# First projection columns by quarters, a reordered end, pairwise squares and moved copies in a one-core decoder step

## The chip, the core and the metric

The kernel runs on one core of one Trainium2 chip (trn2). A core has a matrix engine (TensorE, "PE", with its weight loads listed apart as "PEld"), a vector engine (VectorE, "DVE"), a scalar engine (ScalarE, "ACT"), a general engine (GpSimd, "POOL") and a queue that only issues transfers (SyncE, "SP"). Each engine works through its own instructions in order, and they meet through semaphores. ACT and POOL issue transfers as well. The metric is the device time of one execution in microseconds (us); the profiled execution's span, from its first to its last instruction, is a little shorter.

## The reference

One step of a decoder layer over 512 prompt tokens and 32 sample tokens (8 sequences of 4), 544 tokens of 1024 features, all in float32:

```python
h = RMSNorm_pre(x)
[x_r | q | k | v | g] = h @ W_in                 # 1024 -> 1024 + 1024 + 256 + 256 + 2048
A = RG-LRU(causal_conv4(x_r))                    # recurrent branch, gates by 8 diagonal blocks
B = sliding-window(128) attention, 8 query heads, 2 kv heads, sinks, relative bias
m = (sigmoid(g_A) * (A @ W_A) + sigmoid(g_B) * (B @ W_B)) @ W_out
x = x + RMSNorm_post(m)
u = causal_conv3(RMSNorm_pre2(x) @ W_up)         # 1024 -> 8192
x = x + RMSNorm_post2((gelu(u_gate) * u_val) @ W_down)   # 4096 -> 1024
```

It returns the new x of both groups, the recurrent states, the last keys and values, and the last rows before both convolutions.

## The kernel before

Features lie on the 128 partitions and tokens along the free dimension, so an activation is a set of tiles of 128 x 544. Every product is made exact enough by splitting both operands into a high part (ACT rounds it) and a low part (DVE subtracts it), and by three matmuls: high by high, high by low, low by high. Tokens go in two halves: 256 and 288 (`HALF`), from the output projection on 272 and 272 (`HALF2`). A column block is 128 outputs, with 8 blocks of the inner dimension: 24 matmuls for each half.

**The order.** PE, ACT, DVE and POOL instructions run in the order in which the program writes them (in the second part POOL, too, is ordered by a scheduler); SP's are placed by priority. In the mixer `step` makes one half column, and then `tick` advances a clock `now` and emits what is due: generators put in with `start_at(t, ...)`, the results of the step before (`late`), the weight splits that `wclaim` names (ACT part `wsplit_hi`, DVE part `wsplit_lo`), and last the list `last`.

**The start.** POOL builds `ident` and then `ones`; 7 warm-up matmuls (14 passes on PE, L403) use both. The first 256 tokens arrive as four tiles of 128 x 512 and the first weight column in two halves of its inner dimension. `trans_a(z)` (L469) transposes four of the eight feature blocks on PE, `hsplit` (L445, L446) scales and splits them, and `first_step` (L1024) makes the first half column from the first four blocks, then from the other four. `keep_a` and `keep_b` (L454) copy the transposed tokens out, and `trans_b` (L487) brings tokens 256 to 543. The other five of the first six columns follow for half 0, then all six for half 1, then the other six. `ATTN` gives the ticks of the 16 attention units.

**The second norm.** `norm_chain(1, acc)` runs beside the first up-projection products ("pq", with weight splits "wl_e"). In five groups, half a tick apart, it scales two blocks, adds them to x (POOL, or DVE for blocks 5 and 7), squares them on ACT (L1257), and `sum_up` adds seven squares of 128 x 272 one after the other to `accx` on DVE (L174).

**The pairs.** Each of the up-projection's 32 column pairs from 6 on takes seven products of 12 matmuls ("s", a Strassen-like form: a11, a12, p2, p3, p1, p4, a22). Its weight sums are made by DVE and by two adding transfers of POOL (L1433, L1434). Between them stand halves of the down-projection ("dn", q = 0 to 6), at the places that the planner names: behind a12, p3, p1 and a22, and in pairs 29 to 31 behind p1 and a22. A transfer named ("up", p, "s") brings the weights of one pair a second time; for pairs 30 and 31 (`APART_S`) it goes into two slots from the pool of 52 (L1402).

**The end.** The last quarter of the down-projection (`QL`) runs for half 1 and then half 0. `last_done` adds the result, squares it on ACT (L1775) and collects the squares. `b_sums`, `b_scale`, `b_spread`, `b_norm`, `rows` and `b_out` norm half 1 beside half 0's products and write it out by token blocks 2 to 4. For half 0, `last_sums` and `last_newton` give the row scale, and `a_out` (L1828) scales, adds the tokens of before and writes; its block (1, 1) goes by ACT (L1832) and POOL (L1833).

Of the kernel before, what the change touches and what calls it, by code (L numbers as in the profile page):

```python
# [17 lines left out]
P = 128  # L18
# [34 lines left out]
APART_S = 30  # L53
E_BUFS = 5
# [4 lines left out]
NORM_TICKS = (3, 1.5)  # L59
# [64 lines left out]
def hawk_step(ctx, tc, I, O):  # L124
# [87 lines left out]

    ident = keep.tile([P, P], F32, name="ident")
    make_identity(nc, ident)
    ones = keep.tile([P, P], F32, name="ones")
    pool.memset(ones, 1.0)
# [14 lines left out]
    qkv_order = (16, 18, 8, 9, 10, 11, 17, 19, 12, 13, 14, 15)  # L231
# [8 lines left out]
    in_slots = {("out", c) for c in range(3, 8)} | {("in", c) for c in qkv_order[3:FIRST]}  # L240
    wraw, wunits, wnext = {}, {}, [0]
# [4 lines left out]
    def wraw_parts(i, us):  # L246
        for u in us:
            nc.sync.dma_start(out=wraw[i][:, 4 * u:4 * u + 4, :], in_=wsrc(order[i])[:, 4 * u:4 * u + 4, :])

    def wload(i, halves=None):  # L250
        key = order[i]
        raw = wraw[i] = rp.tile([P, KD, P], F32, tag="raw", name="raw_" + wname(i))
        if halves is not None:
            wraw_parts(i, halves)
        elif key[0] == "wg":
# [33 lines left out]

    def upto(key, a, look):  # L290
        return 2 * (wpos[key] + look) + a + 1
# [29 lines left out]
    def mmhalf(ps, key, X, a, ks=range(KD), js=range(3)):  # L321
        n = X.half[a][1] - X.half[a][0]
        if key == order[0]:

            for j, (i0, i1) in enumerate(((0, 0), (0, 1), (1, 0))):
                if j not in js:
                    continue
                for k in ks:
                    mm(ps[:, :n], wunits[2 * wpos[key] + k // 4][i0][:, k % 4, :], X.get(k, a, i1),
                       j == 0 and k == 0, j == 2 and k == KD - 1)  # L330
            return
        for k in ks:
            wh, wl = (wunits[2 * wpos[key] + k // 4][j][:, k % 4, :] for j in range(2))
            xh, xl = X.get(k, a, 0), X.get(k, a, 1)
            mm(ps[:, :n], wh, xh, k == 0, False)
            mm(ps[:, :n], wh, xl, False, False)
            mm(ps[:, :n], wl, xh, False, k == KD - 1)
# [34 lines left out]

    relx = cp.tile([NBK + 1, NH], F32, name="relx")
    ohp = T("ohp")[:NBK + 1, 0:3 * WIN]
    pool.memset(relx, 1.0)
    xload(0, 0)
    xload(1, 0)
    wload(0, (0,))
    xload(0, 1)
    xload(1, 1)  # L380
    wraw_parts(0, (1,))
    wload(1)
    nc.sync.dma_start(out=ohp, in_=I["c_ohp"])
    nc.sync.dma_start(out=relx[0:NBK, :], in_=I["rel_bias"])
    wload(2)
    for z in range(2):
        for i in (2, 3, 4):
            xload(i, z)
        wload(3 + z)
    wload(5)  # L390
# [12 lines left out]
    for z in range(WARM):  # L403
        mm(pw[:, (z % 4) * P:(z % 4 + 1) * P], ones, ident, True, True)
# [14 lines left out]
    for k in range(KD):  # L419
        h.alloc(k)  # L420
    ss = cp.tile([P, 4, 5], F32, name="ss")
    dve.memset(ss, 1.0)
# [7 lines left out]
    def xsquares(i, zs=(0, 1)):  # L430
        n = TOK[i][1]
        for z in zs:
            xb = xt[i, z][:n, 0:512]
            if z == 0:
                act.activation(jk[:n, 0:512], xb, AF.Square, accum_out=ss[:n, 0, i:i + 1])
            else:
                dve.scalar_tensor_tensor(out=jv[:n, 0:512], in0=xb, scalar=1.0, in1=xb, op0=ALU.mult,
                                         op1=ALU.mult, accum_out=ss[:n, 1, i:i + 1])

    def xtile(i, k):  # L440
        return xt[i, k // 4][:, (k % 4) * P:(k % 4 + 1) * P]
# [22 lines left out]
    def trans_a(z):  # L464
        for i in range(2):
            for j in range(4):
                if j not in pta:
                    pta[j] = (PM if j == 3 else PX)(f"ps_ta{j}")
                pe.transpose(pta[j][:, z * 256 + i * P:z * 256 + (i + 1) * P], xtile(i, 4 * z + j), ident)  # L469

    def split_a(z, ks):
        for j in ks:
            hsplit(4 * z + j, 0, pta[j][:, z * 256:(z + 1) * 256])

    def keep_a(j):
        xkeep(slice(j, KD, 4), 0, 256, pta[j][:, 0:512], act.copy if j % 2 else dve.tensor_copy)
# [6 lines left out]
    def trans_b(ks):  # L483
        for k in ks:
# [3 lines left out]
            hsplit(k, 1, ps[:, :288])  # L488
        for k in ks:
            keep_b(k)  # L490

    def side_b():
        for ks in (range(0, 3), range(3, 6), range(6, 8)):
            last.append(lambda ks=ks: trans_b(ks))
            yield
        yield
        xspill()

    def roots():
        add(ss[:, 0, :], ss[:, 0, :], ss[:, 1, :])  # L500
# [6 lines left out]
    def row_scales():  # L507
        last.extend(lambda i=i: xsquares(i, (1,)) for i in range(2))
        yield 2
        last.append(lambda: xsquares(2))  # L510
        yield
        last.extend(lambda i=i: xsquares(i) for i in (3, 4))
        yield
# [164 lines left out]
    def kv_done(kv, a, ps, nm, scaled):  # L678
# [5 lines left out]
        if a == 1:  # L684
# [3 lines left out]
            late.append(scale)  # L688
# [305 lines left out]

    start_at(3, side_b())
    start_at(3, row_scales())
    start_at(4, once(xspill))
    start_at(2, row_loads())
    start_at(3, attn_tables())
    start_at(9, params())  # L1000
    start_at(14, cache_shift())
    for hp in range(4):
        start_at((7, 12, 19, 27)[hp], once(load_btab, hp))
    start_at(12, sample_tables())
# [19 lines left out]
    def first_step():  # L1024
        key = order[0]
        ps = PM("pm_first")
        def parts(z):
            split_a(z, range(1))
            lows = [wsplit_hi(w) for w in wclaim(z + 1)]
            split_a(z, range(1, 4))  # L1030
            for v in lows:
                wsplit_lo(*v, pool)

        k03, k47 = range(4), range(4, 8)
        trans_a(0)
        parts(0)
        for i in range(2):
            xsquares(i, (0,))
        mmhalf(ps, key, h, 0, k03, (0, 1))
        trans_a(1)  # L1040
        parts(1)
        mmhalf(ps, key, h, 0, k03, (2,))
        mmhalf(ps, key, h, 0, k47)
        last.extend(lambda j=j: keep_a(j) for j in range(4))
        tick(6)
        late.append(lambda: in_done(qkv_order[0])(0, ps))

    first_step()
    table_loads()
    for z, c in enumerate(qkv_order[:FIRST]):  # L1050
        if z:
            step(("in", c), h, 0, in_done(c), target=min(2 * z + 6, 2 * FIRST))
    for z, c in enumerate(qkv_order[:FIRST]):
        step(("in", c), h, 1, in_done(c), target=2 * FIRST + (0, 2, 4, 6, 6, 6)[z])
    for c in qkv_order[FIRST:]:
        for a in range(2):
# [165 lines left out]
    def norm_chain(a, acc):  # L1222
# [8 lines left out]
        with tc.high_priority(offset=HP):  # L1231
# [12 lines left out]
            def sum_up(c):  # L1244
                add(acc2[:, :n], acc2[:, :n], sq[c][:, :n])

            for g in range(5 if a else 0):
# [7 lines left out]
                for c in range(2 * g - 2, 2 * g) if g else ():  # L1255
# [646 lines left out]
```

## Time and profile before

| | |
|---|---|
| median of 3 runs | 996.52 us (996.49 to 996.71) |
| profiled execution, its own time | 996.34 us |
| its span | 994.6 us |
| mean granted PE clock | 0.997 |
| HBM read, written | 111.30 MB, 11.37 MB |
| kernel's share of PE on the chain that ended last | 87% |

The page lists busy time per engine, the chain of work that ended last (followed back from the last instruction), groups of instructions, and transfers. Other views of the same trace give instructions in order of time, waits by pair of engines, and the busy time in any stretch. Ends of PE's instructions are modelled, so a busy PE says less than the starts of its instructions do. A row of the timeline gives start, duration, engine, line, operation, tiles, shape and count, and in brackets the idle time before it with what ended that.

### The profile page before, as it was taken

Reading aid. Unit: us, or ns where it says so; the run is one execution under the profiler, and the core shown is the slowest. Engines: PE = TensorE matmul, PEld = TensorE weight load, DVE = VectorE, ACT = ScalarE, POOL = GpSimd, SP = SyncE. Lnnn points to the kernel's source line nnn. Section 1 sums busy time; section 2 is a strip of 40 time slices with the busy share of each in tenths; the row PEclk is TensorE's granted clock in tenths of the full one; section 3 lists DMA queues with packets and bytes.
Section 4 is the critical chain, followed back from the end, with each engine's and each line's share of the span. In section 5 each row is a group of like instructions: output and inputs, shape, how many; then the busy total and the mean of one; then the engine's idle time right before and its main releaser. Section 6 shows DMA issues by size and latency. Waiting matters only on the chain.

```text
span 994.6 us, 20258 instructions
## 1 busy us (share of the span) xinstructions
PE 981.9 (99%) x7819; PEld 973.3 (98%) x7819; DVE 732.4 (74%) x1547; ACT 596.3 (60%) x1450; POOL 147.4 (15%) x270
## 2 busy tenths in 40 slices
PE   8999999999999999999999999999999999999996
PEld 7999999999999999999999999999999999999996
DVE  5766666685766755589966778787878787879855
ACT  6555556665778635556956655555565655556644
POOL 4242000120101441220001010101010101011003
PEclk9999999999999999999999999999999999999998
DMA  9943223342223634235037586868685868577412
GB/s 269 277 161 94 64 68 105 97 116 64 86 85 86 196 113 140 74 117 165 23 96 180 139 178 141 179 141 180 139 180 140 182 136 182 138 181 196 146 46 91
DMA packets 209236, 134.00 MB, mean 135 GB/s; under 512 B 6696, under 2 KB 195513, under 8 KB 209108
## 3 DMA queue, kind: packets, MB, share of 16 engines
q1 hardware_dynamic: 198548, 110.08, 39.2%
q0 software_dynamic: 10240, 20.08, 11.7%
q10 hardware_dynamic: 352, 2.56, 0.6%
q8 instruction: 61, 1.00, 0.4%
q14 instruction: 35, 0.29, 0.1%
HBM read 111.30 MB, written 11.37 MB: 123 GB/s over the span
## 4 chain that ended last, share of the span: by engine, by line
PE 87%; issue 4%; DVE 4%; DMA 2%; ACT 1%; POOL 1%; POOLq 0%; SPq 0%; DVEq 0%; ACTq 0%
PE pmin L165 22%; PE pmdn L165 18%; PE pux L1513 15%; PE puy L1513 7%; PE pq L1513 6%; PE pmlo L165 4%; PE puz L1513 4%; PE pmao L165 3%; PE pg L165 1%; PE psc L165 1%; PE pvp L165 1%; PE pmout L165 1%; DMA raw_up_s<-in_w_up_dram 1%; DMA raw_up_s<-raw_up_s 1%; DVE accx L174 1%
## 5 line engine op out<-in xcount | busy, mean ns | idle before, releaser
L165 PE MATMUL pmin<-hH,wh_in 128*128 128x256 f32 (+1 forms) x568 | 165.3, 293 | 0.0
L165 PE MATMUL pmin<-hH,wl_in 128*128 128x256 f32 (+1 forms) x568 | 162.8, 289 | 0.3 <-DVE wl_in L288 0.3
L165 PE MATMUL pmin<-hL,wh_in 128*128 128x256 f32 (+1 forms) x568 | 162.5, 288 | 0.0
L165 PE MATMUL pmdn<-fH,wh_dn 128*128 128x256 f32 (+1 forms) x512 | 148.2, 289 | 0.0
L165 PE MATMUL pmdn<-fH,wl_dn 128*128 128x256 f32 (+1 forms) x512 | 147.4, 288 | 0.0
L165 PE MATMUL pmdn<-fL,wh_dn 128*128 128x256 f32 (+1 forms) x512 | 147.3, 288 | 0.0
L165 PEld LDWEIGHTS pmin<-hH,wh_in 128*128 128x128 f32 x568 | 106.9, 189 | 1.3 <-ACT wh_in L283 0.6
L165 PEld LDWEIGHTS pmin<-hL,wh_in 128*128 128x128 f32 x568 | 106.9, 189 | 0.0
L165 PEld LDWEIGHTS pmin<-hH,wl_in 128*128 128x128 f32 x568 | 106.4, 188 | 0.5 <-DVE wl_in L288 0.5
L177 DVE SCALAR_TENSOR_TENSOR uc<-u,fv,uc 128x560 f32<-128x560 f32 x128 | 101.8, 797 | 0.8 <-ACT uc L1544 0.5
L165 PEld LDWEIGHTS pmdn<-fH,wh_dn 128*128 128x128 f32 x512 | 96.5, 189 | 0.1
L165 PEld LDWEIGHTS pmdn<-fL,wh_dn 128*128 128x128 f32 x512 | 96.4, 188 | 0.1
L165 PEld LDWEIGHTS pmdn<-fH,wl_dn 128*128 128x128 f32 x512 | 96.3, 188 | 0.0
L174 DVE TENSOR_TENSOR ft<-ft,pmdn 128x256 f32<-128x256 f32 (+1 forms) x112 | 48.7, 435 | 27.8 <-PE pmdn L165 27.8
L1639 ACT COPY u<-pux 128x272 f32<-128x272 f32 x52 | 20.1, 386 | 80.9 <-PE pux L1513 80.8
L168 DVE TENSOR_TENSOR u<-puy,u 128x240 f32<-128x240 f32 (+2 forms) x78 | 24.6, 344 | 48.5 <-PE puy L1513 31.2
L288 DVE TENSOR_TENSOR wl_in<-raw_in,wh_in 128x512 fp32r<-128x512 f32 x70 | 46.7, 685 | 3.6 <-ACT wh_in L283 3.6
L1544 ACT ACTIVATE uc<-u,fv 128x560 f32<-128x560 f32 x64 | 48.3, 755 | 0.9 <-DVE u L1520 0.9
L168 DVE TENSOR_TENSOR wl_dn<-raw_dn,wh_dn 128x512 fp32r<-128x512 f32 x64 | 43.8, 685 | 4.5 <-ACT wh_dn L1445 4.5
L283 ACT ACTIVATE wh_in<-raw_in 128x512 fp32r<-128x512 f32 x72 | 43.9, 626 | 4.4 <-DMA raw_in<-in_w_in_dram 3.9
L1445 ACT ACTIVATE wh_dn<-raw_dn 128x512 fp32r<-128x512 f32 x64 | 39.7, 623 | 3.0 <-DMA raw_dn<-in_w_down_dram 3.0
L165 PE MATMUL pmout<-mH,wh_out 128*128 128x272 f32 x128 | 37.5, 293 | 0.0
(753 smaller groups left out, 3290.4 us busy)
## 6 DMA issues: line engine op xcount, KB each, us to landing
raw_in<-in_w_in_dram SPq DMA_DIRECT2D x35, 512.0 KB, 4.3
raw_dn<-in_w_down_dram SPq DMA_DIRECT2D x56, 256.0 KB, 3.6
raw_up_s<-in_w_up_dram SPq DMA_DIRECT2D x24, 512.0 KB, 5.7
raw_up_s<-raw_up_s POOLq DMA_DIRECT2D x26, 256.0 KB, 5.4
raw_ao<-in_w_attn_o_dram SPq DMA_DIRECT2D x8, 512.0 KB, 3.9
raw_lo<-in_w_lru_o_dram SPq DMA_DIRECT2D x8, 512.0 KB, 3.8
raw_out<-in_w_out_dram SPq DMA_DIRECT2D x8, 512.0 KB, 5.2
x<-xtd SPq DMA_DIRECT2D x8, 272.0 KB, 6.0
```

What stands on the lines that cost most here:

```text
L165: pe.matmul(out, l, r, start=start, stop=stop)
L168: dve.tensor_tensor(out=out, in0=a, in1=b, op=ALU.subtract)
L174: dve.tensor_tensor(out=out, in0=a, in1=b, op=ALU.add)
L177: dve.scalar_tensor_tensor(out=out, in0=a, scalar=s_, in1=b, op0=op0, op1=op1)
L283: act.activation(hl[0], raw, AF.Copy)
L288: (eng or dve).tensor_tensor(out=hl[1], in0=raw, in1=f32(hl[0]), op=ALU.subtract)
L1445: act.activation(hl[0], src, AF.Copy)
L1513: pe.matmul(ps[:, :HN], w, x, start=start and k == 0 and i == 0, stop=stop and k == 3 and i == 2, skip_group_check=True)
L1544: act.activation(yt[j][:, 0:FLATU], u[:, 0:FLATU], AF.Copy, scale=fv[:, j:j + 1])
L1639: act.copy(e[nm_], z)
```

## The change

1. **Start.** `ones` is made before `ident`, and 6 warm-up matmuls use `ones` alone. The first four projection columns (16 to 19: both keys, both values) are made together for half 0 by quarters of the inner dimension: four transfers of 128 x 2 x 256 for the tokens and four of 128 x 2 x 512 for the weights alternate. For each quarter the four columns' products run part by part, with the next quarter's transposes between them. Three further warm-up matmuls stand behind the first transposes. The first query column then gets half 0 alone, and then half 1 follows for these five columns. Scaling of keys and values gets ticks of its own (`KV_TICK`), the squares of tokens go to `sq4`, and the ticks of the attention units and tables move.
2. **Second norm.** Squares are added by pairs of blocks, 544 wide, and the two halves of the sum at the end.
3. **Last pairs.** The planner's places for pairs 29 to 31 become three, three and one; pair 30's second copy of weights is issued by ACT behind product p3 of pair 28 rather than by SP; three loads of the down-projection go to the slots.
4. **End.** Half 1's last square is added on DVE, so that the column sums take one operand, and they run in the middle of the second product of half 0. Norming, transposes and output of half 1 come one or two steps earlier; the order of the last transposes and outputs is new; the samples' rows leave by ACT's queue.

```diff
+PLACES = (("a12", "p3", "p1", "a22"), ("a12", "p3", "p1"), ("a12", "p3", "p1"), ("a12",))
-NORM_TICKS = (3, 1.5)
+NORM_TICKS = (3, 1)
-FIRST = 6
-ATTN = (10, 12, 14, 16, 18, 20, 22, 24, 26, 28, 30, 32, 34, 36, 38, 40)
+GROUP = (16, 17, 18, 19)
+ATTN = (13, 15, 16, 18, 20, 21, 23, 25, 27, 28, 30, 32, 34, 36, 38, 40)
-WARM = 7
+WARM = 6
+FILL = 3
+KV_TICK = 10
...
-qkv_order = (16, 18, 8, 9, 10, 11, 17, 19, 12, 13, 14, 15)
+qkv_order = (*GROUP, *range(8, 16))
...
+    def gload(q):
+        graw[q] = rp.tile([P, 2, 4 * P], F32, tag="raw", name=f"raw_group{q}")
+        nc.sync.dma_start(out=graw[q], in_=w_in[256 * q:256 * q + 256, GROUP[0] * P:(GROUP[0] + 4) * P]
+                          .rearrange("(k p) n -> p k n", p=P))
...
+    for q in range(4):
+        xquarter(q)
+        gload(q)
+    for i in (2, 3, 4):
+        xload(i, 0)
+    wload(4)
+    for i in (2, 3, 4):
+        xload(i, 1)
...
+    def first_group():
+        accs = [(PX if z == 3 else PM)(f"pm_group{z}") for z in range(4)]
+        def prod(q, z, js):
+            mmhalf(accs[z], order[z], h, 0, (2 * q, 2 * q + 1), js)
+        def splits(q):
+            ghigh(q, 1, dve.tensor_copy if q == 0 else act.copy)
+            ghigh(q, 0, act.copy)
+            lows(q)
+            glow(q, 1, dve)
+            glow(q, 0, dve if q else pool)
+        zs = (2, 3, 0, 1)
+        trans_a(0)
+        warm_up(FILL)
+        highs(0)
+        splits(0)
+        for q in range(4):
+            if q < 3:
+                for z in zs:
+                    prod(q, z, (0,))
+                trans_a(q + 1)
+                highs(q + 1)
+                for z in zs:
+                    prod(q, z, (1,))
+                for z in zs:
+                    prod(q, z, (2,))
+                splits(q + 1)
+                if q == 2:
+                    last.append(lambda: trans_b((0, 1), False))
+                last.append(lambda: keep_a(q))
+                tick(10 if q == 2 else 8)
+                continue
+            for z in zs:
+                prod(q, z, range(3))
+                in_done(GROUP[z])(0, accs[z])
...
-            def sum_up(c):
-                add(acc2[:, :n], acc2[:, :n], sq[c][:, :n])
+            def sum_up(k):
+                add(sq[0], sq[0], sq[k])
+                if k == 3:
+                    add(acc2[:, :n], sq[0][:, 0:n], sq[0][:, n:2 * n])
...
-            for g in range(5 if a else 0):
+            for g in range(6 if a else 0):
...
-                for c in {2: (1,), 3: (2, 3, 4, 5), 4: (6, 7)}.get(g, ()):
-                    sum_up(c)
-                if g < 4:
+                if g > 2:
+                    sum_up(g - 2)
+                if g < 5:
                     yield 0.5
...
-            places = [x for x in todo_ if x[2] in (("p1", "a22") if p_ > 32 - CH else ("a12", "p3", "p1", "a22"))]
+            places = [x for x in todo_ if x[2] in PLACES[max(0, p_ - 28)]]
...
+        if x == ("s", APART_S - 2, "p3"):
+            load(("up", APART_S, "s"), act)
...
+            elif c == 7:
+                add(acc3[1][:, :n], acc3[1][:, :n], sq3[1][7][:, :n])
...
-            down(QL, c, a, last_done(c))
+            down(QL, c, a, last_done(c), b_sums if (a, c) == (0, 1) else None)
...
-    rows(4, 0, PX)
-    rows(0, 0, PM)
+    for i in (2, 3):
+        rows(i, 1, PX)
     while todo:
         slot(0)
-    b_out(4, 0)
+    b_out(2, 1, dve.tensor_copy)
     fin["a"] = last_sums(0, 2, PM("pst_o0"))
-    for i in (2, 3):
-        rows(i, 1, PX)
+    b_out(3, 1)
+    rows(0, 0, PM)
     r = last_newton(*fin["a"])
+    rows(1, 1, PX)
     rows(1, 0, PM)
-    b_out(2, 1)
-    for i in (0, 1):
-        rows(i, 1, PX)
-    b_out(3, 1)
-    a_out(0, 0, r, act)
-    a_out(1, 1, r, nc.sync)
-    a_out(1, 0, r, act)
-    rows(4, 1, PX)
-    b_out(4, 1)
-    a_out(0, 1, r, nc.sync)
+    a_out(0, 0, r)
+    rows(0, 1, PX)
+    a_out(1, 0, r)
+    a_out(1, 1, r)
+    for kk in range(2):
+        rows(4, kk, PX)
+    for kk in range(2):
+        b_out(4, kk)
+    a_out(0, 1, r)
+    for kk in range(2):
+        act.dma_start(out=ys[:, kk * 512:(kk + 1) * 512], in_=fin["o", kk])
```

More of the change, by code (lines that the diff above doesn't have):

```diff
@@ L322, in mmhalf @@
         n = X.half[a][1] - X.half[a][0]
[L323 to L337, printed above, removed]
+        for j_ in (js,) if len(js) == 3 else [(j,) for j in js]:
+            for k in ks:
+                for j, (w, x) in enumerate(((0, 0), (0, 1), (1, 0))):
+                    if j in j_:
+                        mm(ps[:, :n], wpart(key, k, w), X.get(k, a, x), k == 0 and j == 0, k == KD - 1 and j == 2)
     def step(key, X, a, done, target=None, look=2, quick=False):
@@ L402, in hawk_step, with warm_up @@
     ps0 = PX("ps_rows_a0")
-    for z in range(WARM):
-        mm(pw[:, (z % 4) * P:(z % 4 + 1) * P], ones, ident, True, True)
+    def warm_up(n):
+        for z in range(n):
+            mm(pw[:, (z % 4) * P:(z % 4 + 1) * P], ones, ones, True, True)
+    warm_up(WARM)
     pe.transpose(ps0[:, 0:8], rows_a[0:8, :], ident[0:8, 0:8])
@@ L462, in hawk_step, with trans_a, highs, lows @@
     pta = {}
[L464 to L476, printed above, removed]
+    def trans_a(q):
+        pta[q] = PX(f"ps_ta{q}")
+        for z in range(2):
+            for i in range(2):
+                pe.transpose(pta[q][:, z * 256 + i * P:z * 256 + (i + 1) * P], xtile(i, 2 * q + z), ident)
+    def highs(q):
+        for z in range(2):
+            k = 2 * q + z
+            act.activation(h.get(k, 0, 0), pta[q][:, z * 256:(z + 1) * 256], AF.Copy,
+                           scale=pv[:, G_PRE + k:G_PRE + k + 1])
+    def lows(q):
+        for z in range(2):
+            k = 2 * q + z
+            stt(h.get(k, 0, 1), pta[q][:, z * 256:(z + 1) * 256], pv[:, G_PRE + k:G_PRE + k + 1],
+                f32(h.get(k, 0, 0)), ALU.mult, ALU.subtract)
+    def keep_a(q):
+        xkeep(slice(2 * q, 2 * q + 2), 0, 256, pta[q][:, 0:512], act.copy if q % 2 else dve.tensor_copy)
     ptb = {}
@@ L488, in trans_b, with keep_bs @@
             hsplit(k, 1, ps[:, :288])
+        if keep:
+            keep_bs(ks)
+    def keep_bs(ks):
         for k in ks:
             keep_b(k)
[L492 to L497, printed above, removed]
     def roots():
-        add(ss[:, 0, :], ss[:, 0, :], ss[:, 1, :])
+        dve.tensor_reduce(ss[:, 0, :], sq4.rearrange("p z i -> p i z"), AX.X, ALU.add)
         newton_rstd(ss[:, 1, :], ss[:, 3, :], ss[:, 2, :], ss[:, 0, :])
@@ L507, in row_scales @@
     def row_scales():
[L508 to L511, printed above, removed]
+        last.append(lambda: xsquares(0))
+        yield 3
+        for i in (1, 2):
+            last.append(lambda i=i: xsquares(i))
+            yield
         last.extend(lambda i=i: xsquares(i) for i in (3, 4))
-        yield
         last.append(roots)
@@ L687, in scale @@
                 scaled(kv, t_)
-            late.append(scale)
+                yield
+            start_at(KV_TICK + 2 * kv + (nm == "v"), scale())
     def k_scaled(kv, t_):
@@ L1021, in in_done @@
         return lambda a, ps: f(z, a, ps)
[L1024 to L1034, printed above, removed]
-        trans_a(0)
[L1036 to L1046, printed above, removed]
@@ L1048, in hawk_step @@
-    first_step()
-    table_loads()
[L1050 to L1056, printed above, removed]
+    def first_group():
[9 more added lines that the diff above has]
+        zs = (2, 3, 0, 1)
+        trans_a(0)
+        warm_up(FILL)
[20 more added lines that the diff above has]
+                in_done(GROUP[z])(0, accs[z])
+                if z == 3:
+                    keep_bs((0, 1))
+            last.append(lambda: keep_a(q))
+            last.append(lambda: trans_b((2, 3)))
+            tick(10)
@@ L1057, in hawk_step @@
+    first_group()
+    table_loads()
+    c0 = qkv_order[4]
+    ps = PM("pm_first_q")
+    mmhalf(ps, ("in", c0), h, 0, range(4))
+    trans_b((4, 5))
+    mmhalf(ps, ("in", c0), h, 0, range(4, 8))
+    last.append(lambda: trans_b((6, 7)))
+    tick(10)
+    late.append(lambda ps=ps: in_done(c0)(0, ps))
+    for z, c in enumerate(qkv_order):
+        for a in range(1 if z < 5 else 0, 2):
             step(("in", c), h, a, in_done(c))
@@ L1254, in norm_chain @@
                         add(x1_(c), x1_(c), m_)
[L1255 to L1262 removed]
+                if 0 < g < 5:
+                    sq[g - 1] = T(f"sq_x{a}_{g - 1}")[:, 0:2 * n]
+                    for z in range(2):
+                        act.activation(sq[g - 1][:, z * n:(z + 1) * n], x1_(2 * g - 2 + z), AF.Square)
+                if g > 2:
+                    sum_up(g - 2)
+                if g < 5:
                     yield 0.5
@@ L1672, in hawk_step, with down @@
     ft, xtok = {}, {}
-    def down(q, c, a, done):
+    def down(q, c, a, done, mid=None):
         lo, hi = HALF[a]
@@ L1677, in down @@
         for k in range(CH):
+            if k == CH // 2 and mid is not None:
+                mid()
             wh, wl = (usplit["dn", q, c][j][:, k, :] for j in range(2))
```

128 lines of the change are left out of this document (70 added, 58 removed).

## The prediction

> **What bounds the kernel now.** I read the page's head first, then the busy time by stretches of the span (columns: start and end, length, then busy time and count of PE, PEld, DVE, ACT, POOL, granted PE clock, transfer share, GB/s).
>
> ```profile
> span 994.6 us, 20258 instructions
> PE 981.9 (99%) x7819; PEld 973.3 (98%) x7819; DVE 732.4 (74%) x1547; ACT 596.3 (60%) x1450; POOL 147.4 (15%) x270
> 7.00:13.10 6.10, 5.64 (x31) 4.29 (x32) 3.77 (x10) 5.84 (x16) 3.50 (x5) 1.00 1.15 320
> 446.00:449.20 3.20, 2.34 (x19) 2.13 (x19) 2.88 (x7) 2.21 (x6) 0.00 (x0) 1.00 0.80 243
> 510.00:865.00 355.00, 355.00 (x2835) 355.00 (x2834) 290.51 (x582) 214.03 (x530) 36.13 (x42) 1.00 0.70 159
> 865.00:903.00 38.00, 37.38 (x294) 36.73 (x293) 31.47 (x63) 21.10 (x52) 4.31 (x5) 1.00 0.71 166
> 981.70:994.60 12.90, 4.74 (x40) 4.10 (x38) 3.54 (x10) 4.87 (x11) 1.66 (x2) 0.77 0.47 173
> ```
>
> From 510 to 865 PE and its weight loads never stop, so only fewer PE passes or an earlier end can help there. The change takes away almost no passes; time can come only from the four other stretches, where PE stands: the start, the second norm, the last pairs and the tail. I cost these four and nothing else.
>
> **The start.** Rows of the timeline (start, duration, engine, line), with a row of the chain behind them.
>
> ```profile
> 0.74 0.21 POOL masks.py:197 MEMSET ident<- 128x128 f32 x1 [0.29 <-POOLq L1887]
> 1.27 0.20 POOL L216 MEMSET ones<- 128x128 f32 x1
> 1.52 3.35 PE L165 MATMUL ps_warm<-ident,ones 128*128 128x128 f32 x14 [1.52 <-POOL relx L375]
> 5.00 1.41 PE L469 MATMUL ps_ta<-ident,x 128*128 128x128 f32 x8
> 5.48 0.93 PE L469 MATMUL ps_ta<-ident,x 128*128 128x128 f32 x6
> 6.13 0.47 ACT L445 ACTIVATE hH<-ps_ta,pv 128x256 fp32r<-128x256 f32 x1 [3.24 <-PE ps_ta L469]
> 6.50 0.62 ACT L283 ACTIVATE wh_in<-raw_in 128x512 fp32r<-128x512 f32 x1
> 6.63 0.48 DVE L177 SCALAR_TENSOR_TENSOR hL<-ps_ta,pv,hH 128x256 fp32r<-128x256 f32 x1 [1.33 <-ACT hH L445]
> 7.17 1.48 PE L165 MATMUL pm_first<-hH,wh_in 128*128 128x256 f32 x4 [0.75 <-ACT wh_in L283]
> 9.07 1.03 PE L469 MATMUL ps_ta<-ident,x 128*128 128x128 f32 x8
> 12.45 2.50 DVE L288 TENSOR_TENSOR wl_in<-raw_in,wh_in 128x512 fp32r<-128x512 f32 x4
> 13.38 5.70 PE pmin L165 x48
> ```
>
> The first product starts at 7.17, and the half column of 24 products with its second eight transposes lasts until 13.1: 5.93 us. A product in the steady run takes 5.70/48 = 0.119 us, and a transpose 0.109 between starts (an estimate: eight from 9.07 to 9.86, with the loads between them, at 0.10 to 0.13). The same work at that pace is 24 x 0.119 + 8 x 0.11 = 3.7 us. PE's 5.64 busy us hide this, because a modelled end covers short waits; ACT's 5.84 of 6.10 tell it. ACT, with one column's weights and all highs, sets the pace.
>
> After, the same highs serve four columns. Per quarter PE has 24 products and four transposes, 3.3 us; ACT has two highs (0.47) and two weight highs (0.62, 256 of each of two rows), 2.2 us, and half a copy of 0.6; DVE has two lows (0.48) and two weight lows (2.50/4 = 0.63), 2.2 us, with half a copy. So PE sets the pace. The slack is small inside a quarter: the 16 products behind the transposes last 1.9 us, and ACT's 2.2 us must be done by then, though the second weight half is needed 0.5 us later.
>
> When it begins: `ones` is the first memset, so PE starts at about 1.0 in place of 1.52. Twelve passes of 3.35/14 = 0.24 (0.21 between starts) end at 3.7; the four transposes follow the first tokens, at about 4.0 to 4.8; six fill passes end by 6.1; highs and weight highs (0.47 + 0.40, then 0.62 beside DVE's copy) end at about 6.1. First product: 6.1. The group is 96 products, 12 transposes and the six of `trans_b`: 11.4 + 1.3 + 0.65 = 13.4, end 19.5. Before, the same content (72 more products and `trans_b`) ends at 13.1 + 8.57 + 0.65 = 22.3. That is 2.8; I take 0.4 off for the short waits. **Start: 2.4 us**, from 1.0 (waits of 0.35 us at each of four quarters) to 3.0. The moved ticks (`KV_TICK`, `ATTN`, tables) put ACT's and DVE's work later, on engines that are free for 40% and 26% of the span; I cost them at nothing, which is the nearer end, and the other end is one wait like that of the second norm, 0.9.
>
> **The second norm.** Timeline, and one row of the waits (engine, line, from whom: total, times, longest).
>
> ```profile
> 445.48 2.07 DVE L174 TENSOR_TENSOR accx<-accx,sq_x 128x272 f32<-128x272 f32 x4
> 447.47 0.68 DVE L168 TENSOR_TENSOR wl_e<-raw_up__5735,wh_e 128x512 fp32r<-128x512 f32 x1
> 459.96 0.72 DVE L168 TENSOR_TENSOR h2f<-h2f,h2t 128x544 f32<-128x544 f32 x1
> PE pq L1513 <- DVE wl_e L168: 0.9, 1, 0.9
> ```
>
> Four adds of 272 stand on DVE right ahead of the weight low that PE waits for, and PE loses 0.9 to 1.0. After, one pair add stands there: 544 wide, 0.72 by the nearest row, so `wl_e` comes 1.35 us sooner, and the wait with it goes. What is late next is the sum after the last squares: two adds in a row (0.7 + 0.5) with half a tick more, as many slots as before until the norm's matmuls. **Norm: 0.9 us**, from 0.5 to 1.1.
>
> **The last pairs.** Timeline and chain, a row of the transfers' list, waits.
>
> ```profile
> 872.19 2.94 SPq L1402 DMA_DIRECT2D raw_up_s<-in_w_up_dram  x2
> 875.22 8.64 DMA raw_up_s<-in_w_up_dram
> raw_up_s<-in_w_up_dram SPq DMA_DIRECT2D x24, 512.0 KB, 5.7
> 883.89 0.69 DVE L174 TENSOR_TENSOR p<-raw_up_s,raw_up__12120 128x512 f32<-128x512 f32 x1 [2.90 <-DMA raw_up_s<-in_w_up_dram]
> 892.97 7.64 DMA raw_up_s<-raw_up_s
> ACT wh_s_p L1445 <- DMA raw_up_s<-raw_up_s: 2.3, 1, 2.3
> SPq L1402 <- PE pmdn L165: 2.7, 2, 1.5
> ```
>
> SP issues pair 30's second copy ahead of pair 29's, which then takes 8.64 us where the middle one takes 5.7. DVE waits 2.90 us, the adding transfers start that much late, ACT waits 2.3 us at `wh_s_p`, and the PSUM copies behind it hold PE: in the stretch 865 to 903 its loads are idle 38.00 - 36.73 = 1.27 us. After, ACT issues pair 30's copy behind p3 of pair 28, about 11 us later, and the down-projection halves behind a22 are gone from pairs 29 and 30, each of which now has three. The transfer is then 2.9 us sooner, more than ACT's 2.3. The plan keeps its number of halves, so no PE work is added. What can be late next is pair 31: with only one half between its products DVE has about 11.7 of 12 us to do, by its rows in pair 29, and could cost 0.3. Moving the three down loads to the slots is costed at nothing: SP's and the transfer share's 0.71 cover them. ACT's own issue I take at nothing; if a slot is free it is under 1.5 us, within the 3 us of two products, and a rival below has it otherwise. **Pairs: 1.1 us**, from 0.3 to 1.45.
>
> **The end.** Timeline, and what the engines' last instructions did (count, shortest/median/longest in ns, starts).
>
> ```profile
> 968.94 0.72 PE L165 MATMUL pst_o<-ones,acc 128*128 128x1 f32 x6
> 969.53 0.81 PE L165 MATMUL pst_o<-ones,sq_ft 128*128 128x1 f32 x6
> 981.81 1.05 ACT L1825 COPY yo<-pyo 128x512 f32<-128x512 f32 x2
> 982.76 0.43 ACT L1775 ACTIVATE sq_ft<-ft 128x256 f32<-128x256 f32 x1
> 984.10 0.25 ACT L1788 ACTIVATE nst_o<-pst_o,epst 128x2 f32<-128x2 f32 x1
> 986.50 0.69 ACT L1832 ACTIVATE yo_a<-pyo,nst_o 128x512 f32<-128x512 f32 x1 [1.05 <-PE pyo L1819]
> 987.27 1.26 POOL L1833 TENSOR_TENSOR xtok<-xtok,yo_a 128x512 f32<-128x512 f32 x1 [5.17 <-ACT yo_a L1832]
> L1898 POOLq DRAIN  x3: 46/98/6533, 987.2 to 994.3; - x3
> L1898 SPq DRAIN  x3: 7/7/7, 991.1 to 994.0; - x3
> ```
>
> The column sums of half 1 lose one of two operands: six passes, 969.53 - 968.94 = **0.6 us** of PE, between 0.5 and 0.7. Behind the last product (981.70) the last square waits for two copies of output: they take 1.05 us, and the square starts 0.95 after 981.81. In the new order the copies of block 2 and 3 stand behind the square or before it with room. The transposes for block (1, 1) come ahead of its scaling, so that the 1.05 of waiting for `pyo` goes too. POOL's add, 5.57 us behind the last product before, comes at about 3.8: 1.75 sooner. The very end hangs on POOL: its drain ends at 987.24 + 6.53 = 993.77, 5.2 us after its add (988.53), while SP has drained all transfers by 991.1. I take it that these 5.2 us follow POOL's last work. **Tail: 1.7 us**; if they do not, 0; if instead the transfers set the end, 1.2; nothing more than 2.0, since sqrt, Newton and scaling stay.
>
> **The sum:** 2.4 + 0.9 + 1.1 + 0.6 + 1.7 = 6.7 us. The profiled execution took 996.34, so 989.64; the median of the runs stands 0.18 above it, and I give **989.8**. All low ends together are 1.0 + 0.5 + 0.3 + 0.5 + 0 = 2.3 (994.2; 995.1 with a wait of 0.9 at a moved tick), all high ones 3.0 + 1.1 + 1.45 + 0.7 + 2.0 = 8.25 (988.3).
>
> **Rivals.**
>
> [...]
> [...]
> 2. *The transfers bound the start.*
>
> ```profile
> GB/s 0 0 0 0 7 66 348 386 328 266 206 193 127 183 320 297 215 155 187 259 348 325 345 347 338 315 288 298 293 282 287 294 302 327 337 369 335 332 266 263
> ```
>
> These are 40 bins of 0.35 us over the first 14 us. The four quarters are 4 x 0.786 = 3.15 MB. At some 300 GB/s from 2.0 they are there at 12.5, ahead of the last quarter's 16; at the 206 of the weak bins they come by 17.3, and PE loses 2.0: 991.8. Against it: the weak bins lie where SP's issues were few, and the late ones show 300 and more.
> 3. *The end does not follow POOL:* the 5.2 us are a fixed wait that ends with something else; the sum loses 1.7: 991.5.
> 4. *The change doesn't do what it says:* the short waits in the start eat its gain, and pair 31 that of the pairs, so that under 2 us are left: 995 to 996.5.
> 5. *Slower:* ACT executes in order, and stands at the issue of pair 30's copy until the two slots are free; SP stood there 2.7 us in all. On SP nobody waits behind it, on ACT all PSUM copies do. PE has cover for two products, 3.0 us. The wait makes the kernel measurably slower once it is longer than 3.0 + 6.7 + 2.0 = 11.7 us. If the slots come free only at 896, one pair later, the wait is about 12.5 behind 883.7, PE loses 9.5, and the time is 999.3. Against it: in this trace the slots were had by 874.4, and behind p3 they should be free long before.
>
> **How the numbers follow.** Forecast 0.58, clock 0.12, end apart from POOL 0.10, transfers 0.08, doesn't do what it says 0.07, slower 0.05. I count 0.2%, 2.0 us, as what this kernel's measurement can tell: faster is below 994.5. Forecast and rivals 1 to 3 lie there, less 0.01 for two of them together: 0.87. Within 0.2% is 0.08 (rival 4 with that 0.01), slower 0.05. The range runs from all high ends to all low ends, 988.3 to 994.2, and holds rivals 1 to 3; that every part comes out low and a moved tick costs 0.9 as well is left out with rivals 4 and 5, about 0.14 in all.
>
> **What would show it.** Start: first product near 6.1, its group's end near 19.5, ACT below PE in 6 to 19 us; wrong if PE's passes are still 0.21 us apart after 7, or if a quarter waits for a transfer. Norm: no wait of `pq` for `wl_e` near 446. Pairs: pair 29's copy near 5.7 us, PE's loads without idle time until pair 31, ACT's issue under 1.5 us. End: six sum passes, POOL's add 3.8 us behind the last product and POOL's drain 5.2 us behind its end. The forecast is wrong as a whole if a new wait of PE between 20 and 440 appears, where I cost the moved ticks at nothing.

## The result and the profile after

The changed kernel takes 990.07 us (median of 5 runs, 989.79 to 992.24), the kernel before 996.71 (5 runs beside it, 996.49 to 997.10): ratio 0.9933, 95% interval 0.9922 to 0.9945. Forecast were 989.8 us and a range of 988.3 to 994.2.

The head of the page of the changed kernel, and its busy time by stretches (columns as before; the last stretch begins where the last product starts, 0.28 us ahead of its end):

```profile
span 988.3 us, 20243 instructions
PE 979.9 (99%) x7817; PEld 973.3 (98%) x7817; DVE 736.3 (75%) x1555; ACT 596.8 (60%) x1450; POOL 146.8 (15%) x268
...
7.00:13.10 6.10, 6.10 (x54) 6.10 (x54) 5.08 (x9) 3.64 (x9) 1.88 (x2) 1.00 1.06 379
510.00:865.00 355.00, 355.00 (x2832) 355.00 (x2831) 292.61 (x585) 213.16 (x526) 36.13 (x42) 1.00 0.70 157
865.00:903.00 38.00, 38.00 (x305) 38.00 (x304) 32.03 (x66) 23.15 (x55) 4.31 (x5) 1.00 0.72 164
976.79:988.30 11.51, 4.87 (x43) 4.29 (x41) 4.29 (x12) 3.73 (x8) 1.27 (x1) 0.91 0.51 176
```

Between 7.0 and 13.1 us PE now has 54 passes where it had 31, and ACT is down from 5.84 busy us to 3.64: the pace has gone from ACT to PE. Around the last pairs the weight loads have no idle time left (38.00 of 38.00, before 36.73). The tail, counted from the end of the last product as in the prediction, is 11.2 us (977.07 to 988.28) where it was 12.9.

PE is never idle for long, so the span can be accounted for with one measure: the *lead*, how much sooner the same PE instruction starts in the changed kernel than in the trace of before.

| the instruction, with its start in the changed kernel | lead, us | what lies between |
|---|---|---|
| first gate product of the mixer, 219.2 | 2.61 | the start |
| first product of the recurrent output, 328.5 | 2.82 | moved ticks |
| the second norm's first spreading product (`rep_m`), 434.7 | 2.83 | |
| its second one (`rep_f`), 449.8 | 3.43 | the second norm: +0.6 |
| a down-projection product, 498.5 | 3.33 | |
| a down-projection product, 861.4 | 2.77 | the steady stretch: **-0.56** |
| first transposes of the end, 955.3 | 4.09 | the last pairs: +1.3 |
| spreading product of half 1 at the end (`rep_o`), 968.4 | 4.75 | column sums: +0.65 |
| last product, 976.8 | 4.62 | half 0's products with half 1's transposes: -0.13 |
| last transpose, 981.4 | 4.87 | |
| end of the span, 988.3 | 6.3 | the tail, from the last product on: +1.7 |

All four gains are there. One entry was not looked for: in the steady stretch, where both kernels have the same instructions, in the same order on every engine, and PE never stops, the changed one loses half a microsecond.

### The profile page after: what moved, and what is told of

Its sections match the earlier page's. It is cut to its first block, busy times and chain, and to the rows that moved or that the text cites. A ratio compares the mean times of both kernels' runs of the same rounds, so it can differ in the third digit from the quotient of the medians.

```text
span 988.3 us, 20243 instructions
## 1 busy us (share of the span) xinstructions
PE 979.9 (99%) x7817; PEld 973.3 (98%) x7817; DVE 736.3 (75%) x1555; ACT 596.8 (60%) x1450; POOL 146.8 (15%) x268
## 3 DMA queue, kind: packets, MB, share of 16 engines
q0 software_dynamic: 10240, 20.08, 11.9%
## 4 chain that ended last, share of the span: by engine, by line
PE 91%; issue 4%; DVE 3%; ACT 1%; POOL 0%; DVEq 0%; POOLq 0%; ACTq 0%
PE pmin L168 20%; PE pmdn L168 19%; PE pux L1568 16%; PE puy L1568 8%; PE pq L1568 6%; PE pmlo L168 5%; PE puz L1568 4%; PE pmao L168 3%; PE pg L168 1%; PE pm_group L168 1%; PE psc L168 1%; PE pvp L168 1%; PE pmout L168 1%; PE pt L795 1%; DVE hs L993 1%
## 5 line engine op out<-in xcount | busy, mean ns | idle before, releaser
L168 PE MATMUL pmin<-hH,wh_in 128*128 128x288 f32 (+1 forms) x504 | 147.1, 292 | 0.0
L168 PE MATMUL pmin<-hH,wl_in 128*128 128x288 f32 (+1 forms) x504 | 145.3, 288 | 0.3 <-DVE wl_in L285 0.3
L168 PE MATMUL pmin<-hL,wh_in 128*128 128x288 f32 (+1 forms) x504 | 144.9, 288 | 0.0
L168 PEld LDWEIGHTS pmin<-hH,wh_in 128*128 128x128 f32 x504 | 95.0, 188 | 1.3 <-ACT wh_in L280 0.6
L168 PEld LDWEIGHTS pmin<-hH,wl_in 128*128 128x128 f32 x504 | 94.7, 188 | 0.5 <-DVE wl_in L285 0.5
L168 PEld LDWEIGHTS pmin<-hL,wh_in 128*128 128x128 f32 x504 | 95.0, 188 | 0.0
L285 DVE TENSOR_TENSOR wl_in<-raw_in,wh_in 128x512 fp32r<-128x512 f32 x64 | 43.1, 685 | 0.0
L280 ACT ACTIVATE wh_in<-raw_in 128x512 fp32r<-128x512 f32 x64 | 39.5, 627 | 0.6 <-ACT xcH L949 0.6
L1711 ACT COPY u<-pux 128x240 f32<-128x240 f32 (+1 forms) x50 | 11.2, 278 | 44.9 <-PE pux L1568 44.9
```

Source lines behind the costliest of these rows:

```text
L168: pe.matmul(out, l, r, start=start, stop=stop)
L280: act.activation(hl[0], raw, AF.Copy)
L285: (eng or dve).tensor_tensor(out=hl[1], in0=raw, in1=f32(hl[0]), op=ALU.subtract)
L1711: act.copy(*o)
```

## The experiments

Eleven kernels ran, one of them twice. First each part of the change by itself, put into the kernel before.

**The start alone** (part 1 of the change with all its ticks; the rest as before):

```diff
+GROUP = (16, 17, 18, 19)
+WARM = 6
+FILL = 3
+KV_TICK = 10
...
-    first_step()
+    first_group()
```

> Only the start of the change, with the moved ticks. Theory: the lead of 2.6 us that the first stages show in the changed kernel (2.58 at 293 us, 2.82 at 328) is the start's own and reaches the end: 2.4 to 2.9 us faster than before, 0.9972. Rival, the stages meet: an earlier start only waits longer at the second norm and at the last pairs, whose transfers it does not change: under 1.5 us. The steady stretch (510 to 865 us in before) lasts as long as in before within 0.2 us by the theory; if the lead of the changed kernel shrinks there by 0.57 us because of its moved ticks, it does so here too.

Measured: 993.83 us (7 runs, 993.60 to 994.25; before 996.93), ratio 0.9972, interval 0.9961 to 0.9983. The gain is the start's own. But the last part of the expectation came out the other way: its lead falls from 2.64 at 499 us to 2.06 at 862, so the loss in the steady stretch comes with the start. It is spread thin: no interval between two PE starts there is longer than in before by more than 0.012 us.

**The second norm alone:**

```diff
-NORM_TICKS = (3, 1.5)
+NORM_TICKS = (3, 1)
...
+                add(sq[0], sq[0], sq[k])
+                if k == 3:
+                    add(acc2[:, :n], sq[0][:, 0:n], sq[0][:, n:2 * n])
```

> Only the second norm's squares by pairs. Theory: the wait of pq for wl_e (1.01 us) goes, and a new wait of 0.34 us at the matmuls of the norm's sum (pst_f for accx) takes part of its place, so 0.57 us faster, 0.9994; the group of 0.34 us is there in the trace. Rival: all of the 0.9 us that was forecast comes when nothing else is changed (the new wait comes from the earlier start or from transfers of the start), 0.9991.

Measured: 997.00 us, ratio 0.9998 (0.9989 to 1.0007), too small for the runs. The trace has it: the lead rises by 0.62 us across the norm (-0.46 to +0.16; it starts below zero, because the first 14 us of this execution were slower than those of before, see the kernels without the fill), and PE stands 0.39 at `pst_f`. So the new wait belongs to the new order of the adds, and the rival falls.

**The last pairs alone** (places, ACT's issue, and three loads in slots):

```diff
-            places = [x for x in todo_ if x[2] in (("p1", "a22") if p_ > 32 - CH else ("a12", "p3", "p1", "a22"))]
+            places = [x for x in todo_ if x[2] in PLACES[max(0, p_ - 28)]]
...
+        if x == ("s", APART_S - 2, "p3"):
+            load(("up", APART_S, "s"), act)
```

> Only the last pairs: places, ACT's issue of pair 30's second copy, three loads in slots. Theory: the lead between 860 and 935 us grows by 1.3 us and stays: 1.3 us faster, 0.9987. Rival: the gain needs the rest of the change (the later places or an earlier arrival), then under 0.7 us and idle time of PE's loads again near 886 to 902 us.

Measured: 995.88 us, ratio 0.9989 (0.9980 to 0.9998); the lead rises by 1.35 us (-1.27 at 862 to +0.08 at 943), and the loads are never idle. Yet this size is partly the luck of one trace. With the same old pairs, the other kernels lose less than before's profiled execution did; the stretch from 865 to 903 of the kernel with the norm alone:

```profile
865.00:903.00 38.00, 37.85 (x299) 37.36 (x298) 31.50 (x63) 21.32 (x52) 4.30 (x5) 1.00 0.71 167
```

Its loads are idle 0.64 us, those of the start alone and of the end alone 0.61 each, where before had 1.27. Of the 1.3 us some 0.65 is therefore what three executions in four had to lose, and the rest a worse passage in the one that I worked from. The runs' own interval, 0.2 to 2.0 us, can't tell the two sizes apart.

**The end alone** (part 4 of the change):

```diff
+        ts = (acc3[1],) if a else (acc3[0], sq3[0][7])
...
-            down(QL, c, a, last_done(c))
+            down(QL, c, a, last_done(c), b_sums if (a, c) == (0, 1) else None)
```

> Only the end: one operand of the column sums of half 1, their place, the order of the last transposes and outputs. Theory: 0.6 us in PE at the sums, 0.1 in the last transposes and 1.4 behind the last product, 2.1 us faster, 0.9979, with POOL's last drain ending 5.2 us behind its last add. Rival: the end hangs on the transfers, and POOL's drain ends at another distance from its add (differing by 0.5 us or more): under 1.5 us faster.

Measured: 994.66 us, ratio 0.9978 (0.9969 to 0.9987), as expected. POOL's long drain ends at 991.33, 5.24 us behind its add (986.09), so the rival falls. The four parts sum to 0.28 + 0.02 + 0.11 + 0.22 = 0.63%, the whole change is 0.67%: within these intervals of 0.1% to either side the parts add up.

These traces also settle that the steady stretch's loss isn't noise. Between 499 and 862 us the leads of the kernels with the old start stay as they are to 0.01 us (norm alone 0.16 and 0.16, pairs alone -1.27 and -1.27, end alone -0.47 and -0.47), and the two with the new start, this one alone and the whole change, lose 0.58 and 0.56.

Then the changed kernel with one thing undone or altered.

**The second copy's issue back on SP,** and **the old places** (places only behind p1 and a22 in pairs 29 to 31, ACT's issue kept):

```diff
-            load(("up", APART_S, "s"), act)
```

```diff
-            places = [x for x in todo_ if x[2] in PLACES[max(0, p_ - 28)]]
+            places = [x for x in todo_ if x[2] in (("p1", "a22") if p_ > 32 - CH else ("a12", "p3", "p1", "a22"))]
```

> The changed kernel with pair 30's second copy issued by SP as before, the new places kept. Theory: SP issues it ahead of pair 29's copy again, that copy takes 8 us or more, and PE's weight loads are idle 0.5 to 0.7 us in the 38 us around it, as in the four profiles with the old pairs (0.61 to 0.64 in three, 1.27 in the one of before): 0.6 us slower than the changed kernel. Rival: the new places alone give the slack, idle time 0.1 or less and the same time.

> The changed kernel with the old places of the down-projection halves (four behind pairs 29 and 30 counted by the old rule) and ACT's issue kept. Theory: pair 29's copy takes about 5.7 us, PE's weight loads show no idle time in the 38 us around it, the same time as the changed kernel within 0.2 us. Rival: the places carry the gain: idle time of 0.4 us or more, or the end of the pairs later by that.

Measured: 990.36 us (4 runs, 989.82 to 990.47) and 990.85 (990.49 to 992.13). Their rows for the pairs, SP's issue first:

```profile
865.00:903.00 38.00, 38.00 (x304) 38.00 (x303) 32.03 (x66) 23.11 (x56) 4.30 (x5) 1.00 0.72 163
```

```profile
865.00:903.00 38.00, 38.00 (x302) 37.71 (x301) 31.77 (x67) 22.56 (x55) 5.15 (x6) 1.00 0.77 178
```

My theory falls in the first, and the rival holds: with SP's issue ahead of pair 29's copy nothing is idle. In the second it is right in part. With ACT's issue and the old places 0.29 us is idle, about half of the 0.61 to 0.64 of the old pairs, and the lead falls 0.36 us against the changed kernel, a little less than the rival's 0.4. So the new places alone do the whole; ACT's issue alone does half, and beside the new places it adds nothing. The second adding transfer of that passage and its reader show why; the timeline of before (first fence), of the kernel with SP's issue and the new places, with the issue of pair 29's copy and the DVE sum that reads it (second), and of the kernel with ACT's issue and the old places, its DVE sum ahead (third):

```profile
892.97 0.86 POOL L1434 DMA_DIRECT2D raw_up_s<-raw_up_s  x1 [3.68 <-DMA raw_up_s<-raw_up__12120]
900.64 0.63 ACT L1445 ACTIVATE wh_s_p<-raw_up_s 128x512 fp32r<-128x512 f32 x1 [2.26 <-DMA raw_up_s<-raw_up_s]
```

```profile
872.71 0.78 SPq L1466 DMA_DIRECT2D raw_up_s<-in_w_up_dram  x1
881.48 0.68 DVE L177 TENSOR_TENSOR p<-raw_up_s,raw_up__12142 128x512 f32<-128x512 f32 x1
888.57 0.85 POOL L1489 DMA_DIRECT2D raw_up_s<-raw_up_s  x1 [3.80 <-DMA raw_up_s<-raw_up__12142]
899.09 0.62 ACT L1500 ACTIVATE wh_s_p<-raw_up_s 128x512 fp32r<-128x512 f32 x1
```

```profile
879.66 0.69 DVE L176 TENSOR_TENSOR p<-raw_up_s,raw_up__12121 128x512 f32<-128x512 f32 x1 [1.28 <-DMA raw_up_s<-in_w_up_dram]
897.02 0.63 ACT L1499 ACTIVATE wh_s_p<-raw_up_s 128x512 fp32r<-128x512 f32 x1 [1.70 <-DMA raw_up_s<-raw_up_s]
```

From the issue to the reader 7.7 us pass in the one, and ACT waits 2.26 of them; in the other 10.5 us pass, and nobody waits. In the timeline of PE no half of the down-projection stands behind a12 and p3 there before, and one behind each after: 24 passes more ahead of p1, whose weights these are, 3.0 us, whoever issues the copy. And pair 29's copy, though second in SP's queue again, is no longer waited for: the sum that reads it starts 8.8 us behind its issue without idle time ahead of it. ACT's issue with the old places does bring that copy sooner: DVE waits 1.28 us for it, where it waited 2.72 to 2.90 in the four traces with the old pairs. But ACT's wait for the adding transfer stays, 1.70 us against 1.25 to 2.26.

**No fill:** `FILL = 0` in place of 3, measured twice.

> The changed kernel without the three warm-up matmuls (six passes) behind the first transposes; nothing of the output hangs on them. Theory: PE stands from 4.9 to about 6.1 us, as the old start stands between its transposes and its first product, and there two of four profiles (norm alone, pairs alone) show the passes at half pace again from 8.1 and 8.7 for 3.3 us, the other two do not. So the products of the first 14 us either run at half pace for about 3.4 us (1.5 to 1.7 us slower than the changed kernel) or keep the full pace (same within 0.3), and the time of the runs spreads or rises by up to 1.7 us. Rival: the fill is without effect, because the full pace once granted stays: first products 0.12 us apart from 6.6 on in the profile, and the median is that of the changed kernel within 0.3 us. The steady stretch (510 to 865 us) shows whether its pace follows the number of PE instructions ahead of it: if so it changes by some tenths of a us.

> The kernel without the fill once more, for another profiled execution: its first profile (989.75 us) kept the full pace, and its other three runs took 991.3 to 991.6. Theory: a run takes some 1.6 us more when PE's pause behind the first transposes closes the clock again, so a profiled run of 991.2 or more shows passes 0.21 us apart for about 3.4 us between 7 and 13 us, and one of about 989.8 shows none. Rival: the longer runs lose their time elsewhere, and a profile of 991.2 or more shows the full pace through the first 14 us.

Measured: 991.46 us (989.75, 991.32, 991.60, 991.61), and 989.75 the second time. Both profiled executions took 989.75 and show the full pace from the first product on, so they say nothing of the longer ones. That the clock closes in those stays argued, and that the fill prevents it isn't shown: one run of the changed kernel took 992.24. That the clock can close is shown, in kernels with the old start. The same eight transposes of `first_step`, in the trace of the norm alone and of the end alone (timeline of PE):

```profile
6.72 1.55 PE L165 MATMUL pm_first<-hH,wh_in 128*128 128x256 f32 x4 [0.76 <-ACT wh_in L283]
8.07 1.06 PE L165 MATMUL pm_first<-hL,wh_in 128*128 128x256 f32 x4
8.93 1.91 PE L469 MATMUL ps_ta<-ident,x 128*128 128x128 f32 x8
```

```profile
7.41 1.48 PE L165 MATMUL pm_first<-hH,wh_in 128*128 128x256 f32 x4 [0.50 <-ACT wh_in L283]
8.73 0.74 PE L165 MATMUL pm_first<-hL,wh_in 128*128 128x256 f32 x4
9.31 1.04 PE L469 MATMUL ps_ta<-ident,x 128*128 128x128 f32 x8
```

1.91 us for eight against 1.04: in the first the passes are at half pace again. The granted clock that the trace records is full from 4.6 us, half from 8.0 and full from 11.4; within the first stretch lie a wait of PE of 0.76 us (row at 6.72) and four products spread over 1.35 us (6.72 to 8.07). With the pairs alone the turns come at 5.1, 8.5 and 11.9, so each stretch lasts 3.4 us in both. The length of the pause does not settle whether the clock falls back: in the first trace without the fill PE waits 1.23 us ahead of its first product at 6.20, in the second it stands for 1.6 us from 4.6, and the full pace stays; the first eight products take 1.19 us in the first of them. What does settle it was not tested.

**No POOL at the end:** block (1, 1) like the other three.

```diff
-        if (i, kk) == (1, 1):
+        if False:
             t_ = S("yo_a")[:, 0:512]
```

> The changed kernel with the last block (1, 1) scaled and added in one DVE instruction like the other three, no ACT scaling and no POOL add. Theory: POOL's last drain ends 5.2 us behind its last work, which is then at 976.7, so it is out of the way; DVE has 0.69 us more, and the end is set by SP's last transfers, some 0.7 later than SP's drain at 986.4: 0.3 to 0.5 us faster than the changed kernel, POOL's long drain ending before 983. Rival: POOL's drain ends where it did whatever POOL did last: no gain, or 0.2 to 0.7 us slower by DVE's fourth block.

Measured: **988.53 us** (988.22 to 988.83), ratio 0.9913 (0.9899 to 0.9928); the kernel with SP's issue, beside it on the same chip, 990.36. What the engines' last instructions did, in the changed kernel and then without POOL's add:

```profile
980.98 1.27 POOL L1898 TENSOR_TENSOR xtok<-xtok,yo_a 128x512 f32<-128x512 f32 x1 [4.32 <-ACT yo_a L1897]
L1965 POOLq DRAIN  x3: 46/98/6543, 980.9 to 988.0; - x3
L1965 SPq DRAIN  x3: 7/7/7, 986.4 to 987.8; - x3
```

```profile
974.46 1.56 POOL L1876 TENSOR_TENSOR ft<-ft,x1r 128x288 f32<-128x288 f32 x2
L1965 POOLq DRAIN  x3: 46/98/6538, 974.7 to 986.1; - x3
L1965 SPq DRAIN  x3: 7/7/7, 985.6 to 985.9; - x3
```

POOL's long drain (the longest of the three, with the first of the start times) ends at 987.49 and 981.2, 5.2 us behind POOL's last work (982.25 and 976.0) in both, as in before. So it follows POOL, and the rival falls. Only the gain was larger than expected: in this profile the lead at the last transpose is 0.64 us more than the changed kernel's, the end 1.9 more, so the tail gives 1.26, and not 0.3 to 0.5. The 0.64 is not the edit's: 0.60 of it is there at 443 us already, in an execution whose clock opened at 4.3 us and not at 6.6. I had counted the fourth DVE block (0.69 us) as a later last transfer; SP's first drain comes 7.4 us behind the start of the last 24 transposes (985.6 and 978.20), no later than the 7.6 with POOL (986.4 and 978.84).

**Places in memory.** For the steady stretch, some places were shifted by one between the mixer and the second part, in PSUM or in SBUF:

```diff
+    for nm in (PM, PX):
+        dve.memset(nm("shift")[:, 0:1], 0.0)
```

```diff
+    for z in range(2):
+        pool.memset(f32(wp.tile([P, 4, P], F32R, tag="w", name=f"shift{z}"))[:, 0, 0:1], 0.0)
+    pool.memset(S("shift_s")[:, 0:1], 0.0)
```

> The changed kernel with one more tile taken from each of the two PSUM pools between the mixer and the second part (a memset of one column in each), so that half of the up-projection's and two thirds of the down-projection's accumulators lie in another bank; SBUF is as it was. The lead of the changed kernel falls by 0.56 us between 510 and 865 us although its instructions there are those of before, and the kernels with the old start agree in that stretch to 0.01 us. Theory (places in PSUM): the pace there changes by 0.1 us or more against the changed kernel. Rival (places in SBUF, or the order of the instructions): it stays within 0.02 us.

> The changed kernel with two weight tiles and one slot taken and set free between the mixer and the second part, so that about a sixth of the weight parts and a fifth of the activations of the steady stretch lie at other places in SBUF; PSUM is as it was. Theory (places in SBUF): the lead between 510 and 865 us changes by 0.05 us or more against the changed kernel. Rival (PSUM, or the order of the instructions): it stays within 0.02 us.

Measured against the changed kernel (990.01 and 990.18 us, one run each): with PSUM shifted the lead is -0.022 at 499 us and -0.021 at 874, no change; with SBUF shifted it goes from +0.11 to -0.10. The order of the instructions is the same on every engine in all three, which leaves it out as a cause. So PE's pace depends on where tiles lie in SBUF, by 0.21 us here with, by my count in the program, about a sixth of the weight parts and a fifth of the activations moved. One execution is enough here, for this stretch repeats to the nanosecond: from the down-projection product at 498.5 to the one at 861.4 the four traces with the old start take 362.370 us each, and the changed kernel's and six of its variants', the one with PSUM shifted among them, 362.931 each. With SBUF shifted it is 363.138. That the new start's 0.56 us is this effect is likely, since the tiles can come free in another order there and so lie at other places; it isn't shown, as no kernel had the new start with the old places.

**The norm half a tick later,** without POOL at the end:

```diff
-NORM_TICKS = (3, 1)
+NORM_TICKS = (3, 1.5)
```

> The changed kernel without POOL at the end (as in the kernel with four DVE blocks) and with the norm's wait of half a tick as before (3, 1.5): the matmuls of the norm's sum come one product of 1.43 us later. Theory: PE's wait of 0.34 us at these matmuls goes, what follows has the room, and the lead behind the norm rises by 0.3 us: 988.2. Rival: the half tick is lost again where the first products of the next stage wait for the normed tokens (0.3 to 1.4 us): 988.5 to 989.9.

Measured: 988.64 us (988.34 to 989.33). The wait at `pst_f` is gone, and the lead rises across the norm, from -0.68 at 443 to -0.36 at 457, and is still -0.36 at 509, so the half tick costs nothing there. By 903 it is -0.46: the steady stretch, which takes 363.001 us here by the measure above, and the pairs take 0.1 back, and 0.2 of the 0.3 us stay. The median shows nothing of it, for 0.3 us is less than the runs' spread.

## Why the prediction was right

**The start** was right in size and place. The first product starts at 6.14 (forecast 6.1), the 96 products end at 19.8 (19.5, with all six transposes), PE sets the pace.

```profile
1.00 2.93 PE L168 MATMUL ps_warm<-ones 128*128 128x128 f32 x12 [1.00 <-POOL ones L217]
4.99 1.49 PE L168 MATMUL ps_warm<-ones 128*128 128x128 f32 x6
6.14 1.44 PE L168 MATMUL pm_group<-hH,wh_group 128*128 128x256 f32 x8
7.41 0.60 PE L492 MATMUL ps_ta<-ident,xq 128*128 128x128 f32 x4
```

2.6 us came by 219, and 2.8 by 328, against 2.4: what I took off for short waits was hardly needed. The size is that of one pair of executions: against the same trace of before, the lead at 219 is 1.8 to 3.1 us in the ten traces with the new start, and -0.4 to -1.3 in the three others with the old one. The clock opened at about 6.6, within the eight passes from 6.14 (1.44 us where the next eight take 1.19), behind four transposes and six fill passes; in the other nine traces with this start it opened between 4.1 and 7.0. The 0.12 that the chances give to the clock stands on nothing that a run shows: by 7.0 us it was open in all ten. The transfers (rival 2) came in time for the quarters, but can set the first product: in the profile of the late norm it started at 7.14, and PE had waited 1.65 us for weights whose transfer came late.

**Against the start** stands the wrong step, "I cost these four and nothing else": the stretch from 510 to 865, where PE never stops, gave back 0.56 us. A PE that is never idle still has a pace, and by the measure above it was 362.931 us with the new start, 362.370 with the old.

**The norm** was right as a mechanism and too large: 0.6 us, not 0.9, though above the lower bound of 0.5. The wait of `pq` for `wl_e` is gone. The waits of the changed kernel around it:

```profile
PEld pst_f L168 <- DVE accx L177: 0.4, 1, 0.4
PE pst_f L168 <- DVE accx L177: 0.2, 1, 0.2
...
444.79 0.71 DVE L177 TENSOR_TENSOR sq_x<-sq_x,sq_x 128x544 f32<-128x544 f32 x1
445.54 0.44 DVE L177 TENSOR_TENSOR accx<-sq_x 128x272 f32<-128x272 f32 x1
```

The two adds named as "late next" were late. I saw them and gave them no price: the last group is half a tick nearer to the norm's matmuls than before, and that is the 0.34 us that the later tick gives back.

**The pairs** came out near the forecast (1.3 for 1.1) by a wrong step: "The transfer is then 2.9 us sooner" because ACT issues it. That alone made the copy's wait 1.3 us in place of 2.9 and took away half of the idle time of a usual passage; it left ACT's wait for the adding transfer as it was. The time between the products decided. The new places, which had the cause, I costed as nothing more than a plan of the same length. Half of the size also came from one bad passage.

**The sums** were right (0.65 for 0.6), but half 0's products behind them gave 0.13 back. **The tail** was right in its mechanism, POOL's drain, and in its size: 1.65 for 1.7. The last product of before, and of the changed kernel:

```profile
981.41 0.29 PE L165 MATMUL pmdn<-fH,wl_dn 128*128 128x256 f32 x1
```

```profile
976.79 0.28 PE L168 MATMUL pmdn<-fH,wl_dn 128*128 128x256 f32 x1
```

POOL's add starts 3.9 us behind its end (980.98 and 977.07; forecast 3.8, before 5.57). This was no luck of one trace: from that end to the span's the four traces with the old end take 12.84 to 12.86 us, and the eight with the new one 11.20 to 11.22.

In sum, measured against forecast: +0.4 us at the start, -0.3 in the norm and -0.1 behind it, -0.56 in the steady stretch, +0.2 in the pairs, -0.1 in the end's products, nothing in the tail. The terms come to 6.3 us by the profiles and 6.6 by the medians, against 6.7. That the time was hit within 0.3 us is partly luck, such errors cancelling. Of the rivals none came: ACT's two issues of pair 30's copy took 0.41 and 0.51 us, with no wait.

## What to carry to other kernels

Before an end is tuned, look at which engine's last instruction ends last: a single late operation of POOL, with a drain that ended 5.2 us behind it, held the end of this kernel, and giving it to DVE brought a further 1.3 us in the tail. Where two edits are made for one wait, undo each alone; here the one that was argued for did half, and the other all of it. And take the size of a stall from several executions: the same old pairs cost 1.27 us in one and 0.61 to 0.64 in three.

## What the runs showed of the hardware

- PE's pace without any wait depends on the places of tiles in SBUF: 0.21 us in 375 us with some of them moved, 0.00 with PSUM banks moved (one execution each).
- The granted clock can fall back within the first 14 us: with the norm alone it did so behind a wait of PE of 0.76 us and four products spread over 1.35 us, and was half from 8.0 to 11.4, with eight transposes in 1.91 us in place of 1.04; a wait of 1.23 us in the first trace without the fill did not bring it down. The runs with the old start spread accordingly wide: 995.01 to 996.99 with the pairs alone, 995.57 to 997.63 with the norm alone, but 993.60 to 994.25 with the new start alone. That the spread has this cause was not shown.
- POOL's long drain at the end ended 5.23 to 5.24 us behind POOL's last work in all fourteen traces, wherever that work stood.
